# Forgetting attention on one Trainium2 core: the output bank's copy moved behind the exponentials, its addition into the next slot, and a third raw weight buffer

## The chip, the cores and the metric

The kernel runs on one core of a Trainium2 chip. Its engines are TensorE (PE in the profile, with its weight loads shown apart as PEld), VectorE (DVE), ScalarE (ACT), GpSimd (POOL) and SyncE (SP), which here issues the transfers. The engines run side by side, each works through its own instructions in order, and they wait for each other on semaphores. The metric is the device time of one execution in microseconds (us); lower is better.

## What is computed

One hybrid decoder layer in float32 for 1024 positions of width 1024: an mLSTM with four heads beside a forgetting attention with eight heads of width 64, an output projection over both, cross-attention into 256 memory tokens, a squared-ReLU MLP, and RMS norms between. The part in which the change lies is the forgetting attention and the output projection:

```python
def forgetting_attention(q, k, v, lf):
    cT = jnp.cumsum(lf, axis=1).transpose(0, 2, 1)
    def block(args):                      # one block of 128 queries
        s = einsum('bqhd,bkhd->bhqk', qi, k) * scale
        s = s + (ci[..., :, None] - cT[..., None, :])
        s = where(causal, s, -inf)
        p = softmax(s, axis=-1)
        return einsum('bhqk,bkhd->bqhd', p, v)
x = x + concatenate([ml_out, fx_out], axis=-1) @ w_out
```

## The kernel before

Every matrix is held as a pair of float32r parts, a high part (ScalarE's rounding copy, line 134) and a low part (VectorE's difference, line 135), and a product is three matmuls (lines 186 to 188). The stages follow each other: projections and the mLSTM heads, then the forgetting attention, then the last part of the output projection, cross-attention, and the MLP.

**The forgetting stage** is written out by hand as a sequence of slots. `slot` (line 1026 on) issues one slot's instructions for all engines inside `in_order`, which chains the instructions of each engine in the order in which they are written; in most slots SyncE's are chained too. So within the stage no engine overtakes, and what is written earlier in a slot stands earlier in its engine's queue. One slot holds, in this order:

- the stores and sinks that the slot before left (`late`) are set aside;
- `x.turn()`: TensorE transposes one column of four softmax blocks into a `tp` bank (two such banks, line 782);
- `y.add()`: TensorE multiplies the values with the low and the high part of a column that was cut in an earlier slot and adds to the bank `ov` (line 801). There is **one** `ov` bank for the whole kernel. Rows 0 to 63 and 64 to 127 of it hold the products with the two parts of the values; their sum is the head's output. `adds` keeps columns back until two are waiting (`LAG`), and a column with `last` set ends a half of a head, 512 queries;
- `t.top(e)`: VectorE finds the row maxima of the scores of the slot before (lines 741 and 744);
- `x.cut()`: ScalarE writes the high part and VectorE the low part of the transposed column (lines 134 and 135), in tiles `r_d`, `r_e` of two buffers each, and every third time in a `w4` tile;
- `fx_close` (line 805 on), if this slot's add ended a half: ScalarE copies rows 64 to 127 of `ov` to a tile `r_c` (line 810), VectorE adds rows 0 to 63 to it and writes `om` (line 811);
- `t.exp(e)`: ScalarE's exponentials of the scores of two slots before (line 756, and line 758 for a row in two parts). They read a `sc` bank and so set it free; there are three such banks;
- `scale()`: VectorE's reciprocals (lines 763, 764) and GpSimd's scaling (line 767);
- one transfer of `fx_step` and one of `mix_step`; `part.score`: TensorE's two score matmuls (lines 734 and 735) into a `sc` bank;
- what `late` left (sinks, lines 885, 138, 956; `raw_load`), then `fx_store` for a half that was closed before;
- steps of the filler: the keys and values of the cross-attention, and from `out_unit` on five of the eight parts of the output projection, at a rate of 4.6 per slot;
- `cut_next`: half of a weight tile is cut into its parts, the high part by ScalarE (line 988), the low part by GpSimd for the first half of a tile and by VectorE for the second (line 989).

In the slot after one that ended a half (`closing`) there are no adds; in the one after that two columns are added, the first of which starts the next half in the same `ov` bank. So TensorE returns to the bank two slots after it left it. There are 16 such closes, two for each head; they are counted from 1 to 16 here.

**The weights of the filler** come in through tiles `wr` of two buffers (`raw_load`, line 969 on). A tile is cut no sooner than three slots after its load was issued (`AGE`), and once its second half is cut the next load is issued, one slot later. The 16 tiles of the keys and values hold 512 KB, the 16 of the output projection (`w_out_a`) 320 KB. `row` is a constant tile of 128 x 1024; in this stage only its first 256 columns (`row_m`) are in use.

After the slots the rest of the filler, the last three parts of the output projection (`w_out_b`) and what follows are ordered by the scheduler and not by hand.

Of the kernel before, what the change touches and what calls it, by code (L numbers as in the profile page):

```python
# [12 lines left out]
ALU = mybir.AluOpType  # L13
# [4 lines left out]
P = 128  # L18
# [3 lines left out]
KT = D // P  # L22
NM = 256
MLH = 4
FXH = 8
FXD = 64
# [18 lines left out]
def hybrid_layer(ctx: ExitStack, tc: tile.TileContext, a: dict, out: bass.AP):  # L45
    nc = tc.nc
    v, s, g = nc.vector, nc.scalar, nc.gpsimd
# [7 lines left out]
    def name(tag):  # L55
        count[0] += 1
        return f"{tag}_{count[0]}"

    def sb(tag, shape, bufs, dt=F32):
        return pool.tile(shape, dt, tag=tag, name=name(tag), bufs=bufs)  # L60

    def act(dt=F32R):
        return sb("act", [P, 8, TH], 7, dt)
# [15 lines left out]
    def w2(tag, n=512, dt=F32, p=P):  # L79
        return sb("r_" + tag, [P, 512], BUFS[tag], dt)[:p, :n]  # L80

    def col(tag, n=1, bufs=3):
        return sb("c_" + tag, [P, 8], bufs)[:, :n]
# [24 lines left out]
    def const(n, shape, dt=F32):  # L108
        return pool.tile(shape, dt, tag=n, name=n, bufs=1)
# [145 lines left out]
    row = const("row", [P, T])  # L255
# [74 lines left out]
    for k in range(KT):  # L330
        if k == 1:
            load(wg_raw, a["w_gate"])
        if k % 2 == 0:
            c = slice(k % 4 * 256, k % 4 * 256 + 512)
# [320 lines left out]
    closing = iter(())  # L655
# [28 lines left out]
    for hd in range(MLH):  # L684
        closing = ml_head(hd, *ready)
# [7 lines left out]
    for _ in range(2):  # L693
        t = act().rearrange("p a b -> p (a b)").rearrange("p (i c) -> p i c", i=4)
# [18 lines left out]
    def fx_step():  # L713
        if coming:
            dst, src = coming.pop(0)
            load(dst.bitcast(F32), src)
# [86 lines left out]
    om = {}  # L803

    def fx_close(hd, hf, ov):
        if hd % 2 == 0:
            om[hf] = w2("f")
        rng = slice(hd % 2 * FXD, hd % 2 * FXD + FXD)
        t = w2("c")
        s.activation(t[0:FXD], ov[FXD:], AF.Copy)  # L810
        v.tensor_tensor(out=om[hf][rng], in0=ov[0:FXD], in1=t[0:FXD], op=ALU.add)

    def fx_store(hd, hf):
        if hd == FXH - 1:
# [15 lines left out]
    def score_parts():  # L830

        for hd in range(FXH):
            for hf in range(2):
                if hf:
                    t = act(F32).rearrange("p a b -> p (a b)").rearrange("p (i c) -> p i c", i=4)
                    rooms[hd, hf] = [t[:, d, : (5 + d) * P] for d in range(4)]
                else:
                    t = [w4((P, 2, TH)) for _ in range(2)]
                    rooms[hd, hf] = [t[d // 2][:, d % 2, : (1 + d) * P] for d in range(4)]
                for d in range(4):  # L840
                    x = Tile(hd, 4 * hf + d, rooms[hd, hf][d])
                    for e in range(len(x.parts)):
                        yield x, e
            if hd + 2 < FXH:
                fx_load(hd + 2)
# [6 lines left out]
    def value_steps():  # L852
        fvs = {0: fv_load(0)}
        for hd in range(FXH):
            if hd == FXH - 1:
                mix_fx_in()
            for hf in range(2):
                ov = ov_()
                for j in range(4 * hf + 4):
                    yield Values(hd, hf, j, rooms[hd, hf], fvs[hd], ov)  # L860
                del rooms[hd, hf]
                if hf == 0 and hd + 1 < FXH:
                    fvs[hd + 1] = fv_load(hd + 1)
            del fvs[hd]
# [4 lines left out]
    late = []  # L869
# [96 lines left out]
    sources = [(u, src) for u, (srcs, _) in enumerate(units) for src in srcs]  # L966
# [3 lines left out]
    def raw_load():  # L970
        n = len(raws_)
        if n < len(sources):
            src = sources[n][1]
            raw = sb("wr", [P, 1024], 2)[:, : src.shape[-1]]
            last_raw[:] = [load(raw, src)]
            raws_.append(raw)
            ages.append(now[1])

    def cut_half():

        n, e = divmod(halves[0], 2)
        raw = raws_[n]
        c = raw.shape[-1]
        if e == 0:
            cuts_.setdefault(sources[n][0], []).append(tuple(sb(t, [P, 1024], 3, F32R)[:, :c] for t in ("wh", "wl")))
        hi, lo = cuts_[sources[n][0]][-1]
        c = slice(e * c // 2, (e + 1) * c // 2)
        s.activation(hi[:, c], raw[:, c], AF.Copy)
        (v if e else g).tensor_tensor(out=lo[:, c], in0=raw[:, c], in1=hi[:, c].bitcast(F32), op=ALU.subtract)
        halves[0] += 1  # L990
        if e:
            late.append(raw_load)
# [24 lines left out]
            yield from run(cuts_.pop(u))  # L1017

    parts, steps_, fill = score_parts(), value_steps(), filler()
    scored, exped, adds, ended = [], [], [], []  # L1020
    spent = [0.0]
    LAG, LEAD_, AGE = 2, 13, 3

    stores, topped = [], []

    def slot(values, until):
        with in_order((*COMPUTE, mybir.EngineType.SP) if values or until else COMPUTE):
            now[1] += 1
            todo_ = late[:]
            late.clear()  # L1030
            closing = bool(ended)
            ended.clear()
            x = next(steps_, None) if values else None
            if x:
                x.turn()

            while adds and not closing and len(adds) >= (LAG if x else 1):
                y = adds.pop(0)
                y.add()
                if y.last:  # L1040
                    ended.append((y.hd, y.hf, y.ov))
                    break
            tops = scored[:]
            scored.clear()
            for t, e in tops:
                t.top(e)
            if x:
                x.cut()
                adds.append(x)
            for hd, hf, ov in ended:  # L1050
                fx_close(hd, hf, ov)
                if hd % 2:
                    stores.append((hd, hf, True))
            exps = topped[:]
            topped[:] = tops
            for t, e in exps:
                t.exp(e)
            while exped:
                exped.pop(0).scale()
            exped.extend(t for t, e in exps if e == len(t.parts) - 1)  # L1060
            fx_step()
            mix_step()
            part = next(parts, None)
            if part:
                part[0].score(part[1])
                scored.append(part)
            late.extend(filter(None, [f() for f in todo_]))
            if stores and stores[0][2]:
                stores[0] = (*stores[0][:2], False)
            elif stores:  # L1070
                fx_store(*stores.pop(0)[:2])
            while spent[0] < until:
                step = next(fill, None)
                if step is None:
                    break
                spent[0] += step[0]
                if step[1]:
                    late.append(step[2])
                    break
            if until and cut_next() and spent[0] + 6 < until:  # L1080
                cut_next()
        return x
# [16 lines left out]
    n = 0  # L1099
    while slot(True, max(n - DELAY, 0) * RATE):  # L1100
        n += 1
        if n == 2:
            cut_for(0)
    while adds or late or ended or stores:
        n += 1
        slot(False, (n - DELAY) * RATE)
    now[2] = True
# [470 lines left out]
    for i in range(2):  # L1578
        t = act()
# [14 lines left out]
    def finish(acc, hf, c0, wid, parts):  # L1594

        n = wid // P
        r, var, e, y_, t = (col(c, n) for c in ("r", "var", "den", "y", "t"))
        over = inv[:, 4 * hf + c0 // P :][:, :n]
        v.scalar_tensor_tensor(out=e, in0=over, scalar=EPS, in1=over, op0=ALU.mult, op1=ALU.mult)
        ps = bank()  # L1600
        for i in range(n):
            for k in range(parts):
                nc.tensor.matmul(ps[:, i : i + 1], acc[:, k * wid + i * P :][:, :P], ones, start=k == 0, stop=k == parts - 1)
        v.scalar_tensor_tensor(out=var, in0=ps[:, :n], scalar=1.0 / D, in1=e, op0=ALU.mult, op1=ALU.add)
        g.tensor_tensor(out=y_, in0=var, in1=half[:, :n], op=ALU.pow)
        yield
        v.tensor_tensor(out=t, in0=y_, in1=y_, op=ALU.mult)
        v.scalar_tensor_tensor(out=t, in0=t, scalar=-0.5, in1=var, op0=ALU.mult, op1=ALU.mult)
        v.scalar_tensor_tensor(out=r, in0=t, scalar=1.5, in1=y_, op0=ALU.add, op1=ALU.mult)
        yield  # L1610
        rb = bank()[:, :wid]
        spread(rb, r, n)
        rb = rb.rearrange("p (o c) -> p o c", o=1).broadcast_to([P, 2, wid])
        yield
        for k in range(0, KT, 2):
            y = x2[k // 4][:, k // 2 % 2, :, hf, c0 : c0 + wid]
            v.tensor_tensor(out=y, in0=y, in1=rb, op=ALU.mult)
            load(out[:, k : k + 2, hf * TH + c0 : hf * TH + c0 + wid], y)
            yield
# [83 lines left out]
```

## Time and profile before

| what | value |
|---|---|
| time, median of 3 runs | 1522.78 us (1521.64 to 1523.9) |
| the profiled execution's own time | 1523.35 us |
| its span in the trace | 1521.6 us |
| TensorE busy | 1502.7 us, 99% of the span |
| VectorE, ScalarE, GpSimd busy | 1100.3, 727.7, 510.1 us |
| the chain that ended last | TensorE 93%, VectorE 3%, ScalarE 2%, DMA 1% |
| granted TensorE clock | 0.998 |
| line 810, ScalarE's copy of the bank | 16 times, 596 ns median, first 403.6, last 603.2 us |
| `w_out_a` loads in the stage | 16 times 320 KB |

The profile names an instruction by engine, line, operation and tiles (output<-input). In the timeline each row is the start, the duration, the engine, the line, the operation, the tiles and their shapes; square brackets hold how long the engine stood idle before it and what ended that. In the list of waits a row is: who waited for whom, total us, times, longest. A matmul's end is modelled, so the recorded durations of neighbours overlap. The forgetting stage runs from about 395 to 605 us of the span.

### The profile page before, as it was taken

To read this page: it belongs to the slowest core of one execution; us is meant where nothing else is said; L and a number is where in the kernel's file an instruction comes from. 1 tells how busy PE (TensorE), PEld (TensorE's weight loads), DVE (VectorE), ACT (ScalarE), POOL (GpSimd) and SP (SyncE) were. 2 spreads that over 40 slices of the span, in tenths; PEclk is the share of its full clock that TensorE was granted. 3 is DMA by queue.
4 is the path that set the end of the run, shared out by engine and by line. 5 is a ranking of instruction groups with operands and counts; after the bars stand their busy time and mean duration, and the time that the engine had idled before them with its cause. 6 is when DMAs were issued, how large, how long until landed. Compare 5 with 4: busy or idle time off the path is not lost.

```text
span 1521.6 us, 21977 instructions
## 1 busy us (share of the span) xinstructions
PE 1502.7 (99%) x7694; PEld 1261.5 (83%) x7694; DVE 1100.3 (72%) x1743; ACT 727.7 (48%) x1360; POOL 510.1 (34%) x543
## 2 busy tenths in 40 slices
PE   9999999999999999999999999999999999999997
PEld 9988888889999788888888877778787888888887
DVE  7766676765787786944457989898887667787665
ACT  7324343334687665644443456666664621122124
POOL 1003030413364442511110034544555265663322
PEclk9999999999999999999999999999999999999999
DMA  6322223435888886843344437776678777776623
GB/s 239 109 77 87 98 100 114 135 126 157 246 244 267 260 264 230 300 131 124 119 147 157 153 134 277 247 256 242 222 252 286 291 277 276 276 270 248 239 94 111
DMA packets 122538, 299.86 MB, mean 197 GB/s; under 512 B 13614, under 2 KB 28264, under 8 KB 115516
## 3 DMA queue, kind: packets, MB, share of 16 engines
q1 hardware_dynamic: 122428, 298.46, 57.4%
q8 instruction: 60, 0.98, 0.3%
q14 instruction: 50, 0.41, 0.1%
HBM read 199.60 MB, written 98.81 MB: 196 GB/s over the span
## 4 chain that ended last, share of the span: by engine, by line
PE 93%; DVE 3%; ACT 2%; DMA 1%; issue 1%; SPq 0%; DVEq 0%; POOLq 0%; POOL 0%; ACTq 0%
PE tp L186 8%; PE tp L187 8%; PE tp L188 8%; PE m L186 6%; PE sc L186 6%; PE m L187 6%; PE m L188 6%; PE sc L187 6%; PE sc L188 6%; PE mm L186 6%; PE mm L187 6%; PE mm L188 6%; PE ov L186 2%; PE ov L187 2%; PE ov L188 2%; PE ov L801 2%
## 5 line engine op out<-in xcount | busy, mean ns | idle before, releaser
L186 PE MATMUL tp<-act,wl 128*128 128x512 f32 (+1 forms) x440 | 172.9, 393 | 1.2 <-ACT row L1396 0.7
L187 PE MATMUL tp<-act,wh 128*128 128x512 f32 (+1 forms) x440 | 172.1, 391 | 0.0
L188 PE MATMUL tp<-act,wh 128*128 128x512 f32 (+1 forms) x440 | 171.7, 391 | 0.0
L135 DVE TENSOR_TENSOR wl<-wr,wh 128x1024 fp32r<-128x1024 f32 (+2 forms) x95 | 124.5, 1311 | 22.0 <-ACT wh L134 21.4
L134 ACT ACTIVATE wh<-wr 128x1024 fp32r<-128x1024 f32 (+2 forms) x95 | 95.6, 1007 | 75.9 <-PE tp L188 34.7
L186 PE MATMUL mm<-act,wl 128*128 128x512 f32 (+1 forms) x332 | 127.5, 384 | 0.0
L188 PE MATMUL mm<-act,wh 128*128 128x512 f32 (+1 forms) x332 | 127.3, 383 | 0.0
L187 PE MATMUL mm<-act,wh 128*128 128x512 f32 (+1 forms) x332 | 127.2, 383 | 0.0
L186 PE MATMUL m<-act,wl 128*128 128x512 f32 (+1 forms) x308 | 117.7, 382 | 0.5 <-DVE wl L135 0.5
L188 PE MATMUL m<-act,wh 128*128 128x512 f32 (+1 forms) x308 | 117.7, 382 | 0.0
L187 PE MATMUL m<-act,wh 128*128 128x512 f32 (+1 forms) x308 | 117.5, 381 | 0.0
L186 PEld LDWEIGHTS tp<-act,wl 128*128 128x128 f32 x440 | 82.6, 188 | 20.6 <-ACT row L1396 1.2
L188 PEld LDWEIGHTS tp<-act,wh 128*128 128x128 f32 x440 | 82.6, 188 | 18.9
L187 PEld LDWEIGHTS tp<-act,wh 128*128 128x128 f32 x440 | 82.7, 188 | 18.5
L186 PE MATMUL sc<-act,wl 128*128 128x512 f32 (+1 forms) x248 | 97.0, 391 | 1.0 <-DVE wl L135 1.0
L188 PE MATMUL sc<-act,wh 128*128 128x512 f32 (+1 forms) x248 | 96.7, 390 | 0.0
L187 PE MATMUL sc<-act,wh 128*128 128x512 f32 (+1 forms) x248 | 96.6, 390 | 0.0
L1467 POOL TENSOR_TENSOR z<-wr 128x256 f32<-128x256 f32 x56 | 51.7, 944 | 130.6 <-DMA wr<-w_ff2q 116.8
L134 ACT ACTIVATE wh<-z 128x1024 fp32r<-128x1024 f32 (+1 forms) x54 | 55.5, 1028 | 80.8 <-POOL z L1467 58.4
L135 DVE TENSOR_TENSOR wl<-z,wh 128x1024 fp32r<-128x1024 f32 (+1 forms) x54 | 74.3, 1376 | 7.8 <-ACT wh L134 7.6
L134 ACT ACTIVATE w<-wr 128x768 fp32r<-128x768 f32 (+2 forms) x31 | 25.5, 823 | 106.2 <-PE tp L186 33.7
L188 PEld LDWEIGHTS mm<-act,wh 128*128 128x128 f32 x332 | 62.3, 188 | 12.7
(726 smaller groups left out, 4288.4 us busy)
## 6 DMA issues: line engine op xcount, KB each, us to landing
act<-right SPq DMA_DIRECT2D x49, 1024.0 KB
right<-w SPq DMA_DIRECT2D x56, 256.0 KB
wr<-w_ff2q SPq DMA_DIRECT2D x28, 512.0 KB
right<-r_d SPq DMA_DIRECT2D x49, 256.0 KB
right<-r_e SPq DMA_DIRECT2D x49, 256.0 KB
act<-fqk SPq DMA_DIRECT2D x48, 256.0 KB
wr<-w_in SPq DMA_DIRECT2D x20, 512.0 KB
wr<-w_ff SPq DMA_DIRECT2D x20, 512.0 KB
```

Of the source, the lines that this page charges most:

```text
L134: s.activation(hi, src, AF.Copy)
L135: return v.tensor_tensor(out=lo, in0=src, in1=hi.bitcast(F32), op=ALU.subtract)
L186: nc.tensor.matmul(ps, w[1], x[0], start=first, stop=False, skip_group_check=more)
L187: nc.tensor.matmul(ps, w[0], x[1], start=False, stop=False, skip_group_check=more)
L188: nc.tensor.matmul(ps, w[0], x[0], start=False, stop=last, skip_group_check=more)
L801: nc.tensor.matmul(self.ov[:, c0:], self.fv[:, self.j], t[:, c0:], start=self.j == 0 and t is self.p[1], stop=self.last and t is self.p[0])
L1467: g.tensor_tensor(out=o, in0=x, in1=y, op=op)
```

## The change

`fx_close` still issues ScalarE's copy, but it is now called behind the slot's exponentials, and it returns a function `finish` that holds VectorE's addition (and marks the half for `fx_store`). The slot appends it to `closed`, and the next slot calls it behind its `top`s and ahead of its `cut`. The slot without adds is now the one that finds `closed` filled, which is the same slot as before; the store of a half and its write to memory come one slot later, and the loop may take one slot more at its end.

`raw_load` puts every third weight tile of the output projection, from the second on (the 2nd, 5th, 8th, 11th, 14th), in columns 256 to 895 of `row`, and the load of the first one issues the load of the second at once. So three of these tiles can be on their way or waiting instead of two.

```diff
@@ fx_close
         t = w2("c")
         s.activation(t[0:FXD], ov[FXD:], AF.Copy)
-        v.tensor_tensor(out=om[hf][rng], in0=ov[0:FXD], in1=t[0:FXD], op=ALU.add)
+
+        def finish():
+            v.tensor_tensor(out=om[hf][rng], in0=ov[0:FXD], in1=t[0:FXD], op=ALU.add)
+            if hd % 2:
+                stores.append((hd, hf, True))
+
+        return finish
@@ raw_load
-            raw = sb("wr", [P, 1024], 2)[:, : src.shape[-1]]
+            c, m = src.shape[-1], n - len(sources) + 2 * KT
+            raw = row[:, NM : NM + c] if m > 0 and m % 3 == 1 else sb("wr", [P, 1024], 2)[:, :c]
             last_raw[:] = [load(raw, src)]
             raws_.append(raw)
             ages.append(now[1])
+            if m == 0:
+                raw_load()
@@ slot
-            closing = bool(ended)
-            ended.clear()
+            closing = bool(closed)
...
             for t, e in tops:
                 t.top(e)
+            while closed:
+                closed.pop(0)()
             if x:
                 x.cut()
                 adds.append(x)
-            for hd, hf, ov in ended:
-                fx_close(hd, hf, ov)
-                if hd % 2:
-                    stores.append((hd, hf, True))
             exps = topped[:]
             topped[:] = tops
             for t, e in exps:
                 t.exp(e)
+            while ended:
+                closed.append(fx_close(*ended.pop(0)))
@@
-    while adds or late or ended or stores:
+    while adds or late or closed or stores:
```

More of the change, by code (lines that the diff above doesn't have):

```diff
@@ L1019, in hybrid_layer @@
     parts, steps_, fill = score_parts(), value_steps(), filler()
-    scored, exped, adds, ended = [], [], [], []
+    scored, exped, adds, ended, closed = [], [], [], [], []
     spent = [0.0]
```

## The prediction

> **What bounds the kernel now.** The page's table of engines comes first.
>
> ```profile
> PE 1502.7 (99%) x7694; PEld 1261.5 (83%) x7694; DVE 1100.3 (72%) x1743; ACT 727.7 (48%) x1360; POOL 510.1 (34%) x543
> ```
>
> TensorE is busy for 99% of the span, and the change leaves its matmuls as they are. So only its gaps can be won, or added to. Next the list of waits, for the window 395 to 607 us, the forgetting stage: the rows of TensorE's weight loads (a matmul's load comes just before it and shows the same wait), and ScalarE's for the weights.
>
> ```profile
> PEld sc L734 <- ACT w L756: 4.2, 6, 1.6
> PEld sc L734 <- ACT act L756: 2.4, 4, 1.3
> ...
> PEld ov L801 <- DVE r_f L811: 0.2, 1, 0.2
> ...
> ACT wh L988 <- DMA wr<-w_out_a: 4.9, 4, 2.2
> ```
>
> TensorE's score matmuls (line 734) wait ten times for an exponential to free a score bank, 4.2 + 2.4 = 6.6 us in all; that is nearly all that the change can win. The last two rows show what else to watch: once, TensorE waited for VectorE's addition (line 811) before it might write the output bank again, and ScalarE stands still for weights. Those 4.9 us are ScalarE's; they count only where TensorE then waits for it.
>
> ```profile
> L810 ACT ACTIVATE r_c<-ov x16: 594/596/601, 403.6 to 603.2; 64x512 f32<-64x512 f32 x16
> ...
> L811 DVE TENSOR_TENSOR r_f<-ov,r_c x16: 670/683/685, 404.2 to 603.9; 64x512 f32<-64x512 f32 x16
> ```
>
> Each close costs ScalarE 0.60 us and VectorE 0.68 us, 16 times. Neither is removed, both are moved.
>
> **Part 1: the copy goes behind the exponentials.** At each close the exponential comes 0.60 us sooner, and a score matmul that waits for it up to 0.60 sooner. Whatever ScalarE does after both is where it was. That is the only gain of this part.
>
> **Part 2: the addition goes behind the next slot's maxima.** TensorE takes up the bank again two slots after the close, and now the addition is late in the slot between. Between old place and new stand VectorE's reciprocals, a sink, a weight cut and the next maxima. Behind the waiting matmul stands all of TensorE, so what it waits here is lost. Close 1, from the timeline (ScalarE's, VectorE's and TensorE's rows):
>
> ```profile
> 404.90 0.62 ACT L988 ACTIVATE wh<-wr 128x512 fp32r<-128x512 f32 x1
> ...
> 405.55 0.76 DVE L989 TENSOR_TENSOR wl<-wr,wh 128x512 fp32r<-128x512 f32 x1 [0.57 <-ACT wh L988]
> 406.23 0.68 DVE L741 TENSOR_REDUCE c_mx<-sc 128x1 f32<-128x512 f32 x1
> 406.83 0.68 DVE L135 TENSOR_TENSOR r_e<-tp,r_d 128x512 fp32r<-128x512 f32 x1
> ...
> 406.10 0.47 PE L801 MATMUL ov<-r_e,w 128*128 128x512 f32 x1
> ```
>
> The addition will stand between the maximum (line 741) and the cut's low part (line 135). If nothing before it moves, it runs from 406.83 for 0.68, to 407.51; TensorE wanted the bank at 406.10 and waits 1.41 us. If VectorE comes 0.68 sooner, because the old addition is gone from ahead of the maximum, it ends at 406.83 and the wait is 0.73. Those are the two ends for each close: the start of that cut less the start of TensorE's first matmul in the bank, and 0.68 more. Here the weight cut (line 989) had waited 0.57 us for ScalarE's line 988, which stands behind both copy and exponential and does not move: the upper end, **1.41**. For the others the row of the cut, then TensorE's; closes 2 and 7 have ScalarE's line 988 before them.
>
> ```profile
> 422.00 0.62 ACT L988 ACTIVATE wh<-wr 128x512 fp32r<-128x512 f32 x1
> ...
> 423.73 0.42 DVE L135 TENSOR_TENSOR w<-tp,w 128x256 fp32r<-128x256 f32 x1
> ...
> 422.84 0.28 PE L187 MATMUL m<-act,wh 128*128 128x256 f32 x1
> 422.95 0.28 PE L188 MATMUL m<-act,wh 128*128 128x256 f32 x1
> ...
> 423.10 0.48 PE L801 MATMUL ov<-r_e,w 128*128 128x512 f32 x1
> ```
>
> ```profile
> 431.95 0.69 DVE L135 TENSOR_TENSOR r_e<-tp,r_d 128x512 fp32r<-128x512 f32 x1
> ...
> 431.60 0.47 PE L801 MATMUL ov<-r_e,w 128*128 128x512 f32 x1
> ...
> 451.30 0.42 DVE L135 TENSOR_TENSOR w<-tp,w 128x256 fp32r<-128x256 f32 x1
> ...
> 451.02 0.48 PE L801 MATMUL ov<-r_e,w 128*128 128x512 f32 x1
> ...
> 477.34 0.42 DVE L135 TENSOR_TENSOR w<-tp,w 128x256 fp32r<-128x256 f32 x1
> ...
> 476.63 0.50 PE L801 MATMUL ov<-r_e,w 128*128 128x512 f32 x1
> ...
> 485.42 0.63 ACT L988 ACTIVATE wh<-wr 128x512 fp32r<-128x512 f32 x1
> ...
> 487.29 0.68 DVE L135 TENSOR_TENSOR r_e<-tp,r_d 128x512 fp32r<-128x512 f32 x1
> ...
> 487.45 0.48 PE L801 MATMUL ov<-r_e,w 128*128 128x512 f32 x1
> ...
> 558.89 0.42 DVE L135 TENSOR_TENSOR w<-tp,w 128x256 fp32r<-128x256 f32 x1
> ...
> 559.01 0.48 PE L801 MATMUL ov<-r_e,w 128*128 128x512 f32 x1
> ```
>
> - Close 2: 0.63 to 1.31. ScalarE's line 988 ends at 422.62 and holds the weight cut as in close 1: **1.31**.
> - Close 3: 0.35 to 1.03. No weight cut stands there, VectorE is packed and moves up: **0.35**.
> - Close 4: 0.28 to 0.96. A weight cut holds it in part: the middle, **0.6**.
> - Close 6: 0.71 to 1.39; VectorE is packed, 0.71. But 2.6 us later TensorE waits for an exponential anyway (479.27, below) and 0.6 of the delay falls into that: **0.1**.
> - Close 7: -0.16 to 0.52, held by line 988 to 486.05: **0.52**.
> - Close 12: -0.12 to 0.56, a weight cut before it: **0.2**.
> - The other nine: TensorE comes back late enough, **0**.
>
> Sum 1.41 + 1.31 + 0.35 + 0.6 + 0.1 + 0.52 + 0.2 = **+4.5 us**. At the lower ends, with nothing below zero, the same seven give 0.73 + 0.63 + 0.35 + 0.28 + 0.1 = 2.1; at the upper ends 1.41 + 1.31 + 1.03 + 0.96 + 0.8 + 0.52 + 0.56 = 6.6. At these closes an earlier exponential wins nothing more: TensorE only arrives sooner at the bank and waits there. The gain of part 1 is left where the bank is free in time:
>
> ```profile
> 479.27 0.39 PE L734 MATMUL sc<-act 128*128 128x256 f32 x1 [0.42 <-ACT w L756]
> ...
> 505.14 0.50 PE L734 MATMUL sc<-act 128*128 128x512 f32 x1 [1.33 <-ACT w L756]
> ...
> 514.28 0.39 PE L734 MATMUL sc<-act 128*128 128x256 f32 x1 [0.34 <-ACT act L756]
> ...
> 531.61 0.50 PE L734 MATMUL sc<-act 128*128 128x512 f32 x1 [0.17 <-ACT w L756]
> ```
>
> A matmul is recorded as longer than the spacing at which the next may follow: 0.28 at a spacing of 0.11 for 256 columns (422.84, 422.95 above). So about 0.2 us more than the bracket is lost at each. Closes 9 and 10 (514.28, 531.61) win 0.55 and 0.4, both below the 0.60 of the copy: **-0.95 us**.
>
> **Part 3: the third raw buffer.** The wait at 505.14 (close 8) is the largest, 1.33 + 0.2. Before it ScalarE stood 2.16 us for a weight tile:
>
> ```profile
> 503.13 0.47 ACT L988 ACTIVATE wh<-wr 128x320 fp32r<-128x320 f32 x1 [2.16 <-DMA wr<-w_out_a]
> ```
>
> ```profile
> 481.67 0.33 SPq L975 DMA_DIRECT2D wr<-w_out_a  x1
> ...
> 488.68 0.54 SPq L975 DMA_DIRECT2D wr<-w_out_a  x1
> ...
> 494.95 0.61 SPq L934 DMA_DIRECT2D z<-mix  x1
> 495.67 0.41 SPq L975 DMA_DIRECT2D wr<-w_out_a  x1
> ```
>
> That tile is the third, issued at 495.67. With three buffers tiles 1 and 2 go out at 481.67 and tile 3 at 488.68, 7 us sooner, and ScalarE's wait goes; with the copy behind the exponential, too, the whole of it: **-1.55 us** (at the least 0.6, the copy alone; at the most that). What comes late next are the transfers behind the extra load:
>
> ```profile
> 480.00:505.00 25.00, 23.47 (x159) 21.02 (x157) 17.99 (x46) 17.24 (x49) 10.40 (x18) 1.00 1.01 299
> ...
> 500.53 0.50 PE L187 MATMUL mm<-z,wh 128*128 128x512 f32 x1 [0.34 <-DMA z<-mix]
> ```
>
> From 480 to 505 us the DMA engines are full (share 1.01, 299 GB/s), and TensorE already waits at 500.53 for the last piece of `mix`, issued at 494.95. One more tile of 320 KB stands ahead of it then, 327,680 bytes at 299 GB/s: **+1.1 us** (between 0, if the piece isn't the last to land, and 1.1). The Trainium skill ("DMA: Bandwidth & Descriptors", Specifications) puts HBM's limit for one core at about 358 GB/s; by it the tile would cost 0.9, an estimate from that page, and the sum would be 0.2 lower. The trace's 299 stays below that limit and is what I use.
>
> The other waits for weights (4.9 - 2.16 us) have no wait of TensorE behind them: nothing. The later stores of a half have slots to spare, and the slot more at the end is filled with output projection: nothing; after it the scheduler may order things anew, which I bound at 1 us either way, the size of the largest terms above.
>
> **Sum.** 4.5 - 0.95 - 1.55 + 1.1 = **+3.1 us**. Against the profiled execution's 1523.35 (1521.6 of span, 1.75 around it) that is 1526.5; that execution lies 0.57 above the median of the runs, 1522.78, so for the median **1525.9**.
>
> **Rivals.**
> 1. *The bank is free in time.* Then part 2 costs nothing, and the exponentials win wherever a wait follows a close: 0.95 and 1.55 as above, and at most 0.60 each at closes 1, 3 and 6, together 4.3. With `mix` hardly later that is -4 us, **1518.8**. It decides if the addition ends before TensorE returns at closes 1 and 2. Against it: at 476.63 TensorE waited for the addition even in its old place, and there are 0.63 us missing at best.
> 2. *VectorE is packed everywhere*: the lower ends, 2.1, and `mix` comes no later: 2.1 - 0.95 - 1.55 = -0.4, **1522.4**. Against it line 988's rows at closes 1, 2 and 7.
> 3. *The upper ends everywhere*, ScalarE's cuts wait for TensorE's late adds (they reuse their tiles), and the buffer saves only the copy's 0.6: 6.6 - 0.95 - 0.6 + 1.1 = +6.2, **1529**.
> 4. *The third buffer does nothing*, because the cuts are held to three units ahead: 4.5 - 0.95 - 0.6 = +3.0, no other time than the forecast's.
>
> **How the numbers follow.** 0.2% is 3.05 us, about what a measurement here can tell from no change: 1519.7 and 1525.8. Forecast with rival 4: 0.55, of which 0.33 lies above 1525.8 and 0.22 below, since the sum stands at the bound. Rival 1: 0.13. Rival 2: 0.18. Rival 3: 0.14. So slower 0.33 + 0.14 = 0.47, same 0.22 + 0.18 = 0.40, faster 0.13. The range leaves out most of rival 1 and the far end of rival 3: 1520.0 to 1529.5.
>
> **What would show it.** Right: a new row of waits, TensorE's line 801 for VectorE's addition, at closes 1, 2, 3, 4 and 7, some 4 us in all; the rows of line 734 shrink from 6.6 to under 3; the 2.16 us row of line 988 goes; the wait for `mix` near 500 grows to over 1 us. Wrong: line 801 without such waits, above all at close 1; or differences outside 395 to 610 us that are larger than within.

## The result, and the profile after

The changed kernel takes 1529.07 us in the median of 7 runs (1527.29 to 1531.13), against 1522.78 us (7 runs, 1521.53 to 1526.58): slower by 0.40%, ratio 1.0040 with a 95% interval of 1.0028 to 1.0052. The profiled execution took 1527.70 us (span 1526.0), 4.35 us more than the one of before. In the code of the changed kernel the addition is line 813, the weight cut lines 997 and 998.

TensorE's busy time is what it was; its share fell.

```profile
PE 1502.9 (98%) x7694; PEld 1261.2 (83%) x7694; DVE 1104.9 (72%) x1743; ACT 726.1 (48%) x1360; POOL 506.6 (33%) x543
```

The list of waits of the changed kernel for 395 to 615 us, TensorE's weight loads (who waited for whom, total us, times, longest):

```profile
PEld ov L801 <- ACT wh L997: 3.4, 2, 1.8
PEld ov L801 <- issue: 2.6, 3, 1.3
PEld ov L801 <- DVE r_f L813: 2.4, 2, 1.3
PEld sc L734 <- ACT w L756: 1.3, 2, 0.6
PEld ov L801 <- ACT w L756: 0.9, 1, 0.9
PEld sc L734 <- ACT act L756: 0.8, 2, 0.5
PEld tp L782 <- DVE r_b L138: 0.7, 1, 0.7
PEld tp L782 <- DVE r_e L135: 0.5, 1, 0.5
```

The score matmuls (line 734) wait 2.1 us instead of 6.6: that part of the change did what it says. In exchange the value matmuls (line 801) wait for the output bank eight times, 3.4 + 2.6 + 2.4 + 0.9 = 9.3 us instead of 0.2. A load that waits for several things is put down to one of them, so three of these rows, six waits, name ScalarE or "issue"; the matmul's own row names the addition in six of the eight. All rows together are 12.6 us, those of before in the same window 8.6; the difference of 4.0 is nearly the profile's 4.35.

How the delay grows is seen from TensorE's first matmul in the bank after each close (closes 1, 2, 3, 4, 6, 7, 9 and 12, in the changed kernel's timeline; the rows of before are in the prediction, but for close 9, where TensorE had started at 516.37):

```profile
407.95 0.47 PE L801 MATMUL ov<-r_e,w 128*128 128x512 f32 x1 [1.38 <-DVE r_f L813]
...
426.64 0.47 PE L801 MATMUL ov<-r_e,w 128*128 128x512 f32 x1 [1.63 <-ACT wh L997]
...
435.43 0.50 PE L801 MATMUL ov<-r_e,w 128*128 128x512 f32 x1 [0.83 <-DVE r_f L813]
...
456.05 0.47 PE L801 MATMUL ov<-r_e,w 128*128 128x512 f32 x1 [1.08 <-issue]
...
482.77 0.51 PE L801 MATMUL ov<-r_e,w 128*128 128x512 f32 x1 [1.11 <-DVE r_f L813]
...
493.68 0.47 PE L801 MATMUL ov<-r_e,w 128*128 128x512 f32 x1 [0.57 <-DVE r_f L813]
...
520.33 0.47 PE L801 MATMUL ov<-r_e,w 128*128 128x512 f32 x1 [0.30 <-DVE r_f L813]
...
563.34 0.47 PE L801 MATMUL ov<-r_e,w 128*128 128x512 f32 x1 [0.57 <-DVE r_f L813]
```

The stage itself began 0.52 us later in this execution, as a row ahead of the first close shows, first before and then after:

```profile
396.17 0.33 PE L782 MATMUL tp<-ident,w 128*128 128x128 f32 x1 [0.52 <-DVE r_b L138]
```

```profile
396.69 0.33 PE L782 MATMUL tp<-ident,w 128*128 128x128 f32 x1 [0.53 <-DVE r_b L138]
```

Each start less its counterpart of before, less that 0.52:

| TensorE is behind by, us | close 1 | 2 | 3 | 4 | 6 | 7 | 9 | 12 |
|---|---|---|---|---|---|---|---|---|
| predicted, the terms added up | 1.41 | 2.72 | 3.07 | 3.67 | 3.77 | 4.29 | 3.29 | 3.09 |
| measured | 1.33 | 3.02 | 3.31 | 4.51 | 5.62 | 5.71 | 3.44 | 3.81 |

Up to close 7 the delay grows to 5.7 us; between closes 7 and 12 TensorE makes up 1.9. At close 6 the two rows aren't alike: the forecast's 0.1 is already less the 0.6 that TensorE gets back 2.6 us later, the measured figure is not.

### The profile page after: what moved, and what is told of

It reads as the page before. It is cut to its first block, busy times and chain, and to the rows that moved or that the text cites. A ratio compares the mean times of both kernels' runs of the same rounds, so it can differ in the third digit from the quotient of the medians.

```text
span 1526.0 us, 21972 instructions
## 1 busy us (share of the span) xinstructions
PE 1502.9 (98%) x7694; PEld 1261.2 (83%) x7694; DVE 1104.9 (72%) x1743; ACT 726.1 (48%) x1360; POOL 506.6 (33%) x543
## 5 line engine op out<-in xcount | busy, mean ns | idle before, releaser
L188 PEld LDWEIGHTS mm<-act,wh 128*128 128x128 f32 x332 | 62.3, 188 | 12.6
```

The source lines that it names most:

```text
L188: nc.tensor.matmul(ps, w[0], x[0], start=False, stop=last, skip_group_check=more)
```

## The experiments

The theory: TensorE waits for the one output bank, because the addition that empties it stands behind the next slot's maxima, and the other two parts win a little. The rivals: the third buffer's load crowds the DMA queue; the copy's new place hurts; or the late addition hurts in another way than through the bank. Each part was first undone or done alone, then the addition and the bank were changed. Every ratio is to the kernel before, run on the same chip in the same session; its medians there were 1522.61 us for the first four experiments below, 1522.11 for the next four and 1522.47 for the last two, so across the table it is the ratios that can be compared.

| kernel | median us | ratio, 95% interval | profiled execution, us | TensorE's weight loads waited, us |
|---|---|---|---|---|
| before | 1522.78 | | 1523.35 | 8.6 |
| changed | 1529.07 | 1.0040, 1.0028 to 1.0052 | 1527.70 | 12.6 |
| late addition alone | 1530.14 | 1.0045, 1.0033 to 1.0057 | 1531.47 | 16.7 |
| copy behind the exponentials alone | 1521.36 | 0.9990, 0.9982 to 0.9999 | 1521.21 | 6.0 |
| third buffer alone | 1522.72 | 1.0000, 0.9991 to 1.0008 | 1522.06 | 7.0 |
| changed, no third buffer | 1528.67 | 1.0034, 1.0022 to 1.0046 | 1527.29 | 12.9 |
| changed, addition ahead of the maxima | 1525.17 | 1.0015, 1.0006 to 1.0024 | 1524.57 | 10.4 |
| changed, ScalarE empties the bank | 1524.79 | 1.0013, 1.0003 to 1.0023 | 1523.65 | 9.5 |
| copy and third buffer | 1522.44 | 1.0003, 0.9994 to 1.0012 | 1522.69 | 7.7 |
| copy, addition behind the reciprocals | 1521.62 | 0.9992, 0.9982 to 1.0001 | 1527.28 | 11.0 |
| copy, earlier mix | 1521.77 | 0.9995, 0.9987 to 1.0003 | 1519.77 | 6.3 |
| copy, buffer, earlier mix | 1521.29 | 0.9994, 0.9985 to 1.0003 | 1521.38 | 7.3 |

The last column is the sum of the rows for TensorE's weight loads in the list of waits from 395 to 615 us of each profile. Its change from the kernel before follows that of the profiled time to within 1.6 us in every row: where these kernels differ by several us, it is by what TensorE waits in this stage. Differences of 1 or 2 us can't be read from it.

### The third buffer undone

```diff
-            c, m = src.shape[-1], n - len(sources) + 2 * KT
-            raw = row[:, NM : NM + c] if m > 0 and m % 3 == 1 else sb("wr", [P, 1024], 2)[:, :c]
+            raw = sb("wr", [P, 1024], 2)[:, : src.shape[-1]]
...
-            if m == 0:
-                raw_load()
```

> The changed kernel with two raw buffers again. Theory (TensorE waits for the output bank because the addition comes late; the third buffer helps): the trace of the changed kernel has eight new waits of line 801, and the waits of the old kernel at 500.5 and 505.1 us (0.6 and 1.6 us by start times) are gone, which I put down to the buffer. So without it slower than the changed kernel by 1 to 2 us, about 1530.5, and 7 to 8 us above the kernel before. Rival (the extra load crowds the DMA queue and is what costs): close to the kernel before, 1523 to 1525.

1528.67 us: neither. The loss stays without the buffer, so the rival falls; but the buffer wins nothing here either, where I had expected 1 to 2 us. In this execution ScalarE hardly waits for a weight tile any more, with two buffers. The list of all engines' waits of this kernel:

```profile
ACT wh L994 <- DMA wr<-w_out_a: 0.2, 1, 0.2
```

That was 4.9 us before. TensorE's wait at close 8 is gone too. The stage comes to these tiles later: TensorE's first product with the last piece of `mix` starts at 506.12 instead of 499.80, while the third tile's load went out at 500.11 instead of 495.67, so the transfers have some 2 us more. I had put the loss of those waits down to the buffer; here they are gone without it. That the delay takes them away is not shown: with the late addition alone (below), no less delay and two buffers, they are all there. In that kernel the third tile's load went out at 503.17, 7.5 us later than before, and TensorE's product came at 506.59, only 6.8 later. What sets the moment of the load stays open.

### The third buffer alone

The edit to `raw_load` in the kernel before, nothing else.

> The kernel before with only the third raw buffer. Theory: faster by 1 to 2 us, about 1521, because ScalarE no longer waits for the third weight tile at 503 us and TensorE's wait at 505.1 shrinks from 1.6 to about 0.6. Rival (the extra load delays the last piece of mix by 1.1 us or crowds the queue): no gain, 1523 to 1527.

1522.72 us, no difference (interval -0.09% to +0.08%). In the profiled execution ScalarE no longer waits for `wr` tiles of `w_out_a` and TensorE's waits fell from 8.6 to 7.0, so both are less here, but the runs show no gain from it. Two of the kernels below have the buffer too, and in their profiles ScalarE waits 1.9 and 2.0 us for the first of these tiles. The third tile's load went out at 489.05 instead of 495.67.

### The copy behind the exponentials, alone

```diff
-            for hd, hf, ov in ended:
-                fx_close(hd, hf, ov)
-                if hd % 2:
-                    stores.append((hd, hf, True))
             exps = topped[:]
             topped[:] = tops
             for t, e in exps:
                 t.exp(e)
+            for hd, hf, ov in ended:
+                fx_close(hd, hf, ov)
+                if hd % 2:
+                    stores.append((hd, hf, True))
```

The addition follows the copy in the same slot.

> The kernel before with ScalarE's copy behind the exponentials and VectorE's addition directly behind it in the same slot; two raw buffers. Theory (the cost is the addition's lateness, not the copy's place): TensorE's waits for the exponentials (6.6 us) shrink by 2 to 3 us, the bank is free 0.7 us later than before and only close 6 waits for it; faster by 1.5 to 2.5 us, about 1520.5. Rival (the copy behind the exponentials is itself what hurts, since it holds VectorE's addition and all behind it): slower by 3 us or more.

1521.36 us, 0.10% faster (0.01 to 0.18%): the direction as expected, a little less than the 1.5 us at the least. The waits of this kernel:

```profile
PEld tp L782 <- DVE r_e L135: 1.6, 3, 0.7
PEld sc L734 <- ACT w L756: 1.3, 2, 0.7
PEld ov L801 <- DVE r_f L811: 1.1, 2, 0.6
...
PEld sc L734 <- ACT act L756: 0.7, 2, 0.5
```

Line 734 is down from 6.6 to 2.0 us. Close 8's wait is gone, with two buffers and no delay. Of the 4.6 some is given back: VectorE now stands for the copy (5.4 us in all, twelve times) and is late with the cut (line 135, 1.6 instead of 0.5), and the bank is waited for twice (1.1 instead of 0.2).

### The late addition, alone

The changed kernel without the third buffer, and `closed.append(fx_close(...))` ahead of the exponentials, so that ScalarE's copy stands where it stood before.

> The kernel before with ScalarE's copy at its old place and VectorE's addition behind the next slot's maxima; two raw buffers. Theory: the same waits of line 801 for the bank as in the changed kernel, 8 to 9 us by start times, of which those at closes 3 and 6 were waits for the exponential before: slower by 6 to 8 us, about 1530. Rival (the bank is not what TensorE waits for): within 2 us of the kernel before.

1530.14 us, 0.45% slower: the whole loss of the change and 1 us more, as the theory has it. Its waits:

```profile
PEld sc L734 <- ACT w L756: 4.3, 5, 2.0
PEld ov L801 <- issue: 4.3, 4, 1.7
PEld ov L801 <- PE tp L782: 3.6, 4, 1.2
PEld sc L734 <- ACT act L756: 3.1, 5, 1.3
```

The waits for the exponentials stay (7.4 us) and 7.9 us for the bank come on top. Close 8's is among the former, behind ScalarE's wait for the third weight tile:

```profile
510.46 0.47 ACT L994 ACTIVATE wh<-wr 128x320 fp32r<-128x320 f32 x1 [2.71 <-DMA wr<-w_out_a]
```

```profile
512.47 0.50 PE L734 MATMUL sc<-act 128*128 128x512 f32 x1 [1.72 <-ACT w L756]
```

The four kernels so far fit together: 1.0045 times 0.9990 times 1.0000 is 1.0035, the changed kernel without the buffer has 1.0034 and with it 1.0040, all within the intervals.

### The addition ahead of the maxima

```diff
+            while closed:
+                closed.pop(0)()
             for t, e in tops:
                 t.top(e)
-            while closed:
-                closed.pop(0)()
```

> The changed kernel with the late addition ahead of the next slot's maxima instead of behind them; all else as changed, three raw buffers. Theory (what TensorE waits for is the moment at which VectorE has emptied the bank): the addition ends one maximum (0.6 to 0.7 us) sooner, so each of the eight waits of line 801 shrinks by up to that: 9.2 us by start times become about 4.5, and the kernel is 3 to 4.5 us faster than the changed one, about 1525. Rival (the slot's order on VectorE, or the one slot that the stores come later, costs): no difference to the changed kernel, 1528 to 1530.

1525.17 us, 3.9 us under the changed kernel: as expected. The order on VectorE at close 1, then TensorE's waits for the bank:

```profile
406.59 0.68 DVE L813 TENSOR_TENSOR r_f<-ov,r_c 64x512 f32<-64x512 f32 x1
407.19 0.67 DVE L741 TENSOR_REDUCE c_mx<-sc 128x1 f32<-128x512 f32 x1
```

```profile
PEld ov L801 <- DVE r_f L813: 1.4, 2, 0.8
PEld ov L801 <- ACT wh L997: 1.4, 1, 1.4
...
PEld mm L187 <- DMA z<-mix: 1.1, 1, 1.1
...
PEld ov L801 <- ACT c_mx L758: 1.0, 1, 1.0
PEld ov L801 <- ACT r_p L134: 0.8, 1, 0.8
...
PEld ov L801 <- ACT w L756: 0.4, 1, 0.4
...
PEld ov L801 <- issue: 0.2, 1, 0.2
```

They fell from 9.3 to 5.2 us: one place in VectorE's queue, one maximum, takes some 0.5 us off each of the eight waits, of which seven are left. In this profile the wait for `mix`, which the changed kernel's had not shown, is there again with 1.1; whether that is because the stage is 4 us less late was not tried.

### ScalarE empties the bank

```diff
         s.activation(t[0:FXD], ov[FXD:], AF.Copy)
+        t2 = w2("c")
+        s.activation(t2[0:FXD], ov[0:FXD], AF.Copy)

         def finish():
-            v.tensor_tensor(out=om[hf][rng], in0=ov[0:FXD], in1=t[0:FXD], op=ALU.add)
+            v.tensor_tensor(out=om[hf][rng], in0=t2[0:FXD], in1=t[0:FXD], op=ALU.add)
```

> The changed kernel, but ScalarE copies both halves of the bank to memory behind the exponentials (0.6 us more of ScalarE at each close), and VectorE's addition, at its late place as in the changed kernel, reads the two copies. Theory (the bank, and not the late addition as such): the bank is free in the slot of the close, the waits of line 801 for the addition go, and the time falls by 5 to 7 us to between 1521.5 and 1524. Rival (the late addition hurts through VectorE's order or the later stores): it stays at 1528 to 1530.

1524.79 us, 4.3 us under the changed kernel, the addition as late as there. So most of what the late addition costs goes through the bank, and not through VectorE's order or the later stores. A remainder stays: the kernel is 0.13% slower than the one before (0.03 to 0.23%), and it did not come down to 1521.5 to 1524. Its waits:

```profile
PEld tp L782 <- DVE r_e L135: 2.2, 3, 1.4
PEld mm L187 <- DMA z<-mix: 2.0, 1, 2.0
...
PEld ov L801 <- ACT r_c L812: 0.8, 2, 0.5
```

The bank is down to 0.8 us, but the cuts are waited for longer (2.2 instead of 0.5), and `mix` 2.0 us. The longest wait for a cut comes after close 1:

```profile
407.77 0.67 DVE L815 TENSOR_TENSOR r_f<-r_c,r_c 64x512 f32<-64x512 f32 x1
408.37 0.68 DVE L135 TENSOR_TENSOR r_e<-tp,r_d 128x512 fp32r<-128x512 f32 x1
```

```profile
409.10 0.66 PE L782 MATMUL tp<-ident,act 128*128 128x128 f32 x4 [0.97 <-DVE r_e L135]
```

The late addition (line 815) stands directly ahead of that cut in VectorE's queue, and the weight cut before both had waited for ScalarE, which the second copy holds up. What each of the two adds was not told apart, so a small cost of VectorE's order is not ruled out.

### Copy and third buffer, without the late addition

> The copy behind the exponentials with the addition directly behind it in the same slot, and the third raw buffer: the changed kernel without the late addition. Theory (the late addition is the whole of the loss; the copy's place wins 1.2 us as measured alone; the buffer takes away two waits of TensorE of 2.2 us in the stage but showed no gain alone): between 1519.5 and 1521.5, no slower than the copy alone. Rival (copy and buffer hurt together, through more ScalarE work at once): 1523 or more.

1522.44 us, as fast as the kernel before and no faster than the copy alone: my figure was 1 us too low. The profile has a wait of 1.6 us for `mix` in it, which the prediction had feared from the buffer. One profile of each kernel doesn't pin it on the buffer: the buffer alone had none, and the next kernel has 3.6 us with two buffers.

### The addition behind the reciprocals

In the kernel with the copy alone, `fx_close` returns the addition, and the slot runs it behind `scale()`.

> The copy behind the exponentials and the addition in the same slot, but behind VectorE's reciprocals, so that they don't wait for the copy; two raw buffers. With the addition directly behind the copy's wait, TensorE waited 1.6 us for VectorE's cut and 1.1 us for the bank. Theory: the first goes and the second stays or grows by 0.2 us a close: about 0.5 to 1 us faster than the copy alone, 1520.5. Rival: the bank comes later still and decides, 1522 to 1524.

1521.62 us (interval of the ratio 0.9982 to 1.0001), not to be told from the 1521.36 of the one with the addition right behind the copy. Undecided between the two. The wait for VectorE's cut, which by the theory goes, is still there: 1.7 us, with the copy alone 1.6.

### The transfers of mix sooner

```diff
-            if u == len(units) - 2 * KT - 3:
+            if u == len(units) - 2 * KT - 5:
                 mix_in(0)
```

in the kernel with the copy alone, and in the one with copy and buffer.

> The copy behind the exponentials with the addition directly behind it (two raw buffers), and the transfers of mix for the first half of the output projection begun two units of the filler sooner. Theory (once the bank is no issue, the next thing late is the last piece of mix in the full DMA queue, 0.3 to 3.6 us in the profiles so far): the wait of line 187 for mix goes, and the time is 0.5 to 1.5 us under the copy alone, about 1520. Rival (that wait is only a shift, and the queue makes the weight tiles late in its place): no difference, 1521.4.

> The same with the third raw buffer. Copy and buffer together were 1.1 us slower than the copy alone, and the profile showed 1.6 us of waiting for mix. Theory (the buffer's load stands ahead of mix in the queue): with mix sooner the buffer's gain shows, 1519 to 1520.5. Rival (the buffer brings nothing in any case): as the one without it, or slower, 1521 to 1523.

1521.77 and 1521.29 us. The wait for `mix` is gone from both profiles. Without the buffer that brought nothing against the copy alone, as the rival said. ScalarE's waits moved from one set of weights to another: 3.0 us for the keys' weights, with the copy alone 0.9, and 1.0 for `w_out_a`, there 5.8. TensorE's sum of waits stayed, 6.3 after 6.0. With the buffer it is 1.2 us under copy and buffer alone, in the direction of the theory but inside the intervals, and above its 1520.5. No kernel here beats the copy alone by more than the measurement can tell.

## Why the prediction was right, and where its sizes were off

**The mechanism was right.** Slower by 3.1 us was forecast with a range to 1529.5, and it came to 6.3, near the upper end. The addition moved behind the maxima takes the bank from TensorE; the kernel with that part alone shows it (+0.45%), and moving the addition one place up or emptying the bank otherwise takes away about two thirds of it. Of the signs named, the waits of line 801 came at the closes named and at 6, 9 and 12 too, 9.3 us where some 4 were forecast (a part of that stands where TensorE had waited for an exponential); line 734 fell to 2.1; the row of 2.16 us is gone; the longer wait for `mix` did not come. Close 1 was nearly exact: the addition ran where it was put, and TensorE started 0.15 us after its end.

```profile
406.53 0.68 DVE L741 TENSOR_REDUCE c_mx<-sc 128x1 f32<-128x512 f32 x1
407.13 0.67 DVE L813 TENSOR_TENSOR r_f<-ov,r_c 64x512 f32<-64x512 f32 x1
```

**The sum, "+3.1 us", came near in the traces by luck.** The starts of the same matmuls of TensorE in the two profiled executions, less the 0.52 us from before the stage, give each term (from 501.35 to 506.96, 505.14 to 509.17, 514.28 to 517.72, 516.37 to 520.33, 531.61 to 535.14 and 559.01 to 563.34, behind close 7):

| term | forecast, us | measured, us |
|---|---|---|
| the bank, closes 1 to 7 | +4.29 | +5.71 |
| the wait for `mix` near 500 | +1.1 | -0.62 |
| the wait at close 8 (505.14) | -1.55 | -1.58 |
| the exponentials at closes 9 and 10 | -0.95 | -1.02 |
| the bank at close 9 | 0 | +0.52 |
| the bank at close 12 | +0.2 | +0.80 |
| sum | +3.1 | +3.8 |

The bank cost 2.5 us more than forecast, and the term for `mix` came out 1.7 us lower, below nothing: one error hides two thirds of the other.

**Part 2, "Sum ... +4.5 us": mis-sized.** Up to close 7 the forecast had 4.3 us, the trace has 5.7. Closes 2 and 4 make 1.0 of the difference: 1.69 and 1.20 measured (the steps of the first table) against 1.31 and 0.6. Closes 6 and 7 together make most of the rest, 1.20 against 0.62; 0.26 of that is there before TensorE comes to close 6, with a wait of 0.43 us for an exponential at 459.94 that no term had. Close 9, put at 0 with eight others, cost 0.52, and close 12, put at 0.2, cost 0.80. The upper end, "0.68 more", is no upper end. It took the weight cut on VectorE at its duration of before, 0.69 and 0.68. In the changed kernel it is this (VectorE at close 2 and close 4, then GpSimd at close 2):

```profile
424.31 1.15 DVE L998 TENSOR_TENSOR wl<-wr,wh 128x512 fp32r<-128x512 f32 x1 [0.26 <-ACT wh L997]
...
425.86 0.68 DVE L813 TENSOR_TENSOR r_f<-ov,r_c 64x512 f32<-64x512 f32 x1
...
453.54 1.15 DVE L998 TENSOR_TENSOR wl<-wr,wh 128x512 fp32r<-128x512 f32 x1
```

```profile
424.16 0.76 POOL L767 TENSOR_SCALAR act<-act,c_den,c_mx 128x512 f32<-128x512 f32 x1 [0.32 <-DVE c_den L764]
424.90 1.12 POOL L767 TENSOR_SCALAR act<-act,c_den 128x512 f32<-128x512 f32 x1
```

At close 2, with the addition gone from ahead of them, the reciprocals come sooner, GpSimd's scaling (line 767) starts sooner, 0.15 us ahead of the cut, and the cut takes 0.46 longer. Before, at the same close, the cut started first and GpSimd paid:

```profile
422.76 1.22 POOL L767 TENSOR_SCALAR act<-act,c_den,c_mx 128x512 f32<-128x512 f32 x1 [0.72 <-DVE c_den L764]
```

The cut reads two operands from memory. The Trainium skill ("SBUF — State Buffer", Who interferes with whom) states that a VectorE instruction with two SBUF inputs contends with a GpSimd instruction that reads SBUF, and that the order of issue decides who blocks. At close 2 the rows agree. At close 4 the recorded starts do not tell who blocks; whether the order of issue is another than theirs, no run here shows. There GpSimd started first before the change as well, by 0.13 us, and paid itself; in the changed kernel it started first by 0.14 us, and VectorE paid (first the two rows of before, then GpSimd's after):

```profile
450.10 1.29 POOL L767 TENSOR_SCALAR act<-act,c_den,c_mx 128x512 f32<-128x512 f32 x1 [0.85 <-DVE c_den L764]
...
450.23 0.68 DVE L989 TENSOR_TENSOR wl<-wr,wh 128x512 fp32r<-128x512 f32 x1
```

```profile
453.40 0.76 POOL L767 TENSOR_SCALAR act<-act,c_den,c_mx 128x512 f32<-128x512 f32 x1 [0.32 <-DVE c_den L764]
```

What the longer cut costs at close 4 can be read from the changed kernel without the third buffer. There the lead was 0.13 us again, the cut took 0.69, and TensorE waited 0.62 us for the bank instead of 1.08:

```profile
454.10 0.69 DVE L995 TENSOR_TENSOR wl<-wr,wh 128x512 fp32r<-128x512 f32 x1
```

```profile
456.15 0.47 PE L801 MATMUL ov<-r_e,w 128*128 128x512 f32 x1 [0.62 <-issue]
```

So a part of the loss, 0.46 us at close 4, is a second-order effect of the same move, and it was there or not with a hundredth of a us in the recorded starts. At close 2 the 0.46 is read from the rows alone.

**Rival 3** gave 1529, and the median is 1529.07, but its conditions don't hold together: close 3 stayed at the lower end (0.29 against 0.35), `mix` cost nothing, and close 8's wait went whole, so that the time fits is luck. Its "ScalarE's cuts wait for TensorE's late adds" did happen, 15.6 us in the stage after 6.8, ahead of close 1's next cut for instance, but TensorE is the later of the two by then. Whether the 0.43 us at 459.94 comes from it was not tried.

```profile
408.69 0.60 ACT L134 ACTIVATE r_d<-tp 128x512 fp32r<-128x512 f32 x1 [1.13 <-PE ov L801]
```

**Part 1, "-0.95 us":** right. In the rows TensorE got back 1.02 us at the exponentials of closes 9 and 10, and about as much in every profile with the copy moved; in the two with the copy in its place, third buffer alone and late addition alone, nothing. By the medians the copy's new place alone measured -1.2 us, and late addition alone against changed without the buffer -1.5, both with wide intervals.

**Part 3, "+1.1 us": failed.** It took the queue at 500 us as in the kernel before, with one more tile in it. In the changed kernel TensorE's wait for `mix` went instead of growing. The 299 GB/s of before was no ceiling of the queue either: in the same 25 us the changed kernel's profile has 315, and that of the addition ahead of the maxima 325.

**Part 3, "-1.55 us": right in size, but not the buffer's alone.** TensorE got back 1.58 us at close 8 in the changed kernel, and the third tile was there in time. So it was in all six profiles with the third buffer, but also in three of the six with two: changed without the buffer, copy alone, and copy with earlier `mix`. Wherever the tile was in time, TensorE got back that 1.58 or 1.59 us, with the copy moved or not. Where it was late and the copy moved (the addition behind the reciprocals), it got back 0.59, the prediction's "at the least 0.6". What makes the tile late with two buffers stays open; there is one profile of each kernel.

**What stays open:** the changed kernel's profiled execution is 1.4 us below its median and that of before 0.6 above. The rows explain the 4.35 us between these two executions, 0.52 of it from before the stage; the 2 us by which the medians differ more were not seen in a trace. The interval of the measured loss reaches from 4.3 to 7.9 us.

## What to carry to other kernels

When an accumulator has a single bank, the instruction that frees it has a due time: the moment at which TensorE comes back to it. Before moving it, read for each use how long TensorE is away, and count everything that will stand between in the freeing engine's queue, at the length that it has next to what then runs beside it. A copy that holds up something urgent may go behind it, but the instruction that frees the bank should not go behind the next slot's work.

Two remedies for one wait are not additive: at close 8 a tile in time was worth 1.58 us with the copy moved or not, and the copy's place counted, with 0.59, only where the tile was late. And a transfer's wait that is gone behind a compute wait may come back with it: `mix` was not waited for in the changed kernel, and was again in both kernels that cut the waits for the bank, for reasons not tried.

## What the runs showed of the hardware that was not expected

- VectorE's low part of a weight cut, 128x512 from two tiles in memory, took 0.69 us alone and 1.15 us where a GpSimd scaling of 128x512 had started 0.15 us sooner; where VectorE started first, GpSimd's scaling took 1.22 instead of 0.76. The recorded starts don't mark the switch at zero: over the twelve profiles, such a scaling that led by 0.12 or 0.13 us took 1.28 to 1.30 us and left the cut at 0.68 or 0.69, and one that led by 0.14 or 0.15 took 0.76 or 0.77 and the cut 1.15 to 1.17.
- The kernel with the addition behind the reciprocals ran from 1518.74 to 1527.28 us in 11 executions. The profiled one is the slowest, 5.7 above the median. In it TensorE waited 3.6 us for `mix` and ScalarE 8.2 us for `w_out_a`, and the granted clock was 0.95 in 480 to 515 us, where the other eleven profiles have 1.00. How these waits differ between executions of one kernel was not traced.
